# Row normalisation on one core: loading the first tile through two queues, and a new cut of the scale that two engines share

## The chip, the cores and the metric

The kernel runs on one core of one Trainium2 chip. The metric is the device time of one execution in microseconds (us). The record calls two kernels the same when they lie within 2% of each other. Smaller differences are read here from the ratio and its 95% interval.

## The reference

```python
def setup_inputs():
    batch, dim = 1024, 4096
    return {"x": np.random.randn(batch, dim).astype(np.float32),
            "axis": -1, "eps": np.float32(1e-12)}

def reference(x, axis, eps):
    norm = np.sqrt(np.sum(x ** 2, axis=axis, keepdims=True) + eps)
    return (x / norm).astype(np.float32)
```

16.78 MB come in and 16.78 MB go out. There is little arithmetic to each byte.

## The kernel before

The 1024 rows are two tiles of 128 partitions x 4 rows x 4096 columns, 8.39 MB each, with 64 KB in every partition. The four rows of a partition are called rows 0 to 3 here. Both loads and both stores go through one queue, that of SyncE.

```python
    for i in range(n_tiles):
        g = RowGroups(nc, io, stats, scratch, D, R, eps_t)
        load = nc.sync.dma_start(out=g.flat(), in_=x_t[i])
        if i == 0:
            first_load_to_front(nc, load.ins)   # ahead of the entry barrier
        groups.append(g)

    for i, g in enumerate(groups):
        g.square_dve(R - 1)          # row 3: VectorE
        g.square_act(0)              # rows 0, 1, 2: ScalarE
        g.norm(0)                    # root on ScalarE, reciprocal on VectorE
        g.scale(0)                   # VectorE
        ...                          # the same for rows 1 and 3
        g.square_act(2)
        g.norm(2)
        if i < n_tiles - 1:
            g.scale_by_both(2)       # tile 0: both engines, cut at 7/8
        else:
            g.scale(2)
        store = nc.sync.dma_start(out=out_t[i], in_=g.flat())
```

```python
    def scale_by_both(self, r):
        cut = 7 * self.D // 8
        rstd = self.rstd[:, r : r + 1]
        self.nc.scalar.activation(out=self.x[:, r, :cut], in_=self.x[:, r, :cut],
                                  func=ACT_F.Copy, scale=rstd)
        self.nc.vector.tensor_scalar_mul(out=self.x[:, r, cut:],
                                         in0=self.x[:, r, cut:], scalar1=rstd)
```

`first_load_to_front` moves the finished instruction into the entry block, ahead of SyncE's drain, and so ahead of the barrier at which the engines meet before the body of the kernel: in the trace this load's issue starts at 0.00 us, the second load's, behind the barrier, at 0.79.

## Time and profile before

| | before |
|---|---|
| time, median of 3 runs | 81.94 us (81.75 to 81.99) |
| span of the profiled execution | 80.2 us |
| VectorE, ScalarE busy | 33%, 37% |
| share of the 16 DMA engines' time in packets | 97.4% |
| first store issued / load 1 landed | 38.99 us / 41.37 us |

The time is about 1.8 us longer than the span, which runs from the first to the last instruction. A transfer counts as landed when all 16 DMA engines have reported; the trace has 16 reports for each. The views behind the table stand in the prediction below, with what is to be seen in them.

### The profile page before, as it was taken

The numbers are of one execution on the slowest core, as the hardware profiler recorded it, in microseconds if no ns is written. First come the engines' busy times: TensorE is split into PE (matmuls) and PEld (weight loads), VectorE is DVE, ScalarE is ACT, GpSimd is POOL, SyncE is SP. The second block draws the span as 40 slices with busy tenths as digits, with TensorE's granted clock in tenths as the row PEclk, the third lists the DMA queues.
The fourth block names the chain that finished last, engine by engine and source line by source line (L and its number), as shares of the span: only waits on it lengthen the run. The fifth ranks groups of instructions, "written<-read, shape, count | busy, mean of one in ns | idle before, by whom it ended". The sixth has DMA issues, their size and how long they took to land.

```text
span 80.2 us, 93 instructions
## 1 busy us (share of the span) xinstructions
DVE 26.7 (33%) x21; ACT 29.7 (37%) x23; POOL 0.2 (0%) x4
## 2 busy tenths in 40 slices
DVE  0000000000099599960039995999200000000000
ACT  6000000000099999989439999950000000000000
POOL 0000000000000000000000000000000000000000
DMA  9099996699996699996699990999991999992990
GB/s 490 33 523 523 523 490 294 261 523 523 523 490 261 294 523 523 523 490 261 294 523 523 523 490 33 523 523 523 523 458 65 523 523 523 523 425 98 523 523 0
DMA packets 576, 33.55 MB, mean 418 GB/s; under 512 B 64, under 2 KB 64, under 8 KB 64
## 3 DMA queue, kind: packets, MB, share of 16 engines
q1 hardware_dynamic: 576, 33.55, 97.4%
HBM read 16.78 MB, written 16.78 MB: 418 GB/s over the span
## 4 chain that ended last, share of the span: by engine, by line
DMA 51%; ACT 10%; DVE 9%; issue 0%
DMA xt<-in_x_dram 51%; ACT sq_act L33 9%; DVE xt L64 9%; ACT rstd L53 1%; DVE rstd L59 0%
## 5 line engine op out<-in xcount | busy, mean ns | idle before, releaser
L33 ACT ACTIVATE sq_act<-xt 128x4096 f32<-128x4096 f32 x6 | 21.7, 3609 | 22.4 <-DMA xt<-in_x_dram 22.4
L42 DVE SCALAR_TENSOR_TENSOR sq_dve<-xt 128x4096 f32<-128x4096 f32 x2 | 8.9, 4426 | 26.4 <-DMA xt<-in_x_dram 26.4
L64 DVE TENSOR_SCALAR xt<-xt,rstd 128x4096 f32<-128x4096 f32 x7 | 16.5, 2353 | 0.2
L72 ACT ACTIVATE xt<-xt,rstd 128x3584 f32<-128x3584 f32 x1 | 3.3, 3283 | 0.2 <-DVE rstd L59 0.2
L53 ACT ACTIVATE rstd<-ssq,eps_t 128x1 f32<-128x1 f32 x8 | 2.1, 290 | 0.1
L59 DVE RECIPROCAL rstd<-rstd 128x1 f32<-128x1 f32 x8 | 1.3, 160 | 2.5 <-ACT rstd L53 2.5
L33 ACT ACT_TABLE_LOAD x1 | 1.3, 1283 | 0.8 <-PEq L258 0.8
L53 ACT ACT_TABLE_LOAD x1 | 1.3, 1283 | 0.0
L33 ACT ACTIVATION_READ_ACCUMULATOR sq_act<-xt 128x1 f32 x6 | 1.1, 187 | 0.0
L78 DVE TENSOR_SCALAR xt<-xt,rstd 128x512 f32<-128x512 f32 x1 | 0.5, 487 | 0.0
L211 DVE MEMSET eps_t<- 128x1 f32 x1 | 0.1, 59 | 0.9 <-PEq L258 0.9
L42 DVE DVE_READ_ACCUMULATOR sq_dve<-xt 128x1 f32 x2 | 0.2, 83 | 0.0
L258 POOL MEMSET const-uint8-127<- 128x1 uint8 x1 | 0.1, 103 | 0.0
L258 POOL MEMSET const-bfloat16-1.0<- 128x1 bf16 x1 | 0.1, 102 | 0.0
L258 POOL MEMSET const-float32-0.0<- 128x1 f32 x1 | 0.1, 99 | 0.2 <-issue 0.2
L258 POOL MEMSET const-float32-1.0<- 128x1 f32 x1 | 0.1, 99 | 0.0
## 6 DMA issues: line engine op xcount, KB each, us to landing
xt<-in_x_dram SPq DMA_DIRECT2D x2, 31.3
out_dram<-xt SPq DMA_DIRECT2D x2, 22.5
```

The lines of the kernel that those rows point to most:

```text
L33: self.nc.scalar.activation(out=sq_a, in_=self.x[:, r], func=ACT_F.Square, accum_out=self.ssq[:, r : r + 1],)
L42: self.nc.vector.scalar_tensor_tensor(out=sq_v, in0=self.x[:, r], scalar=1.0, in1=self.x[:, r], op0=ALU.mult, op1=ALU.mult, accum_out=self ...
L53: self.nc.scalar.activation(out=self.rstd[:, r : r + n], in_=self.ssq[:, r : r + n], func=ACT_F.Sqrt, bias=self.eps_t,)
L59: self.nc.vector.reciprocal(out=self.rstd[:, r : r + n], in_=self.rstd[:, r : r + n])
L64: self.nc.vector.tensor_scalar_mul(out=self.x[:, r], in0=self.x[:, r], scalar1=self.rstd[:, r : r + 1])
L72: self.nc.scalar.activation(out=self.x[:, r, :cut], in_=self.x[:, r, :cut], func=ACT_F.Copy, scale=rstd,)
L78: self.nc.vector.tensor_scalar_mul(out=self.x[:, r, cut:], in0=self.x[:, r, cut:], scalar1=rstd)
L211: nc.vector.memset(eps_t, eps)
L258: nc = _bacc.Bacc("TRN2", target_bir_lowering=False, num_devices=1)
```

## The change

The intent: use both issuing engines for the first tile, so that it arrives sooner, and rebalance the shared scale so that the first store can go out sooner.

```diff
-        cut = 7 * self.D // 8
+        cut = 3 * self.D // 4
...
-            if i.engine == mybir.EngineType.SP and isinstance(i, mybir.InstDrain)
+            if i.engine == load.engine and isinstance(i, mybir.InstDrain)
...
-        load = nc.sync.dma_start(out=g.flat(), in_=x_t[i])
         if i == 0:
-            first_load_to_front(nc, load.ins)
+            half = R * D // 2
+            for queue, part in ((nc.sync, slice(half)), (nc.scalar, slice(half, None))):
+                load = queue.dma_start(out=g.flat()[:, part], in_=x_t[i][:, part])
+                to_front(nc, load.ins)
+        else:
+            nc.sync.dma_start(out=g.flat(), in_=x_t[i])
```

The first half holds rows 0 and 1, the second rows 2 and 3.

More of the change, by code (lines that the diff above doesn't have):

```diff
@@ L80, in scale_by_both, with to_front @@
         )
-def first_load_to_front(nc, load):
+def to_front(nc, load):
     def move(program):
```

## The prediction

So is the term for the added packets in the sum: the sum came to about -0.15 us, and so to 81.8 us, with that term in it; the two terms left to read (-0.2 and -0.05) don't add up to that. That the DMA engines take the two halves packet by packet in turn, on which the landing of the halves and the first rival rest, was an assumption: the trace of before has one queue and can't show it. How the descriptors of the two halves are prepared (second rival) and what the start consists of (third rival) are conjectures too. In the trace of before 16 packets of 65,536 bytes in 2.418 us are 433.7 GB/s; that a second queue leaves this rate as it is was assumed as well.

> **What bounds the kernel now.** I read the page first: the busy shares, the slices, the DMA queue.
>
> ```profile
> span 80.2 us, 93 instructions
> DVE 26.7 (33%) x21; ACT 29.7 (37%) x23; POOL 0.2 (0%) x4
> q1 hardware_dynamic: 576, 33.55, 97.4%
> HBM read 16.78 MB, written 16.78 MB: 418 GB/s over the span
> ```
>
> No compute engine is busy for even two fifths of the span, while the packets fill 97.4% of the time of the 16 DMA engines. Two loads and two stores of 8.39 MB each follow one another on one queue, so this is a copy with arithmetic hidden in it. All that isn't copying is 2.6% of 80.2 us, about 2.1 us; no change that leaves the bytes alone can win more than that.
>
> Next I wanted to know whether the four transfers follow without a hole. The view of tile xt and that of the output give the times from issue to landing:
>
> ```profile
> L219 SPq DMA_DIRECT2D xt<-in_x_dram x2: 333/358/383, 0.0 to 0.8; - x2
> DMA to landing us min/median/max: 22.1/31.3/40.6
> L240 SPq DMA_DIRECT2D out_dram<-xt x2: 343/346/348, 39.0 to 56.8; - x2
> DMA to landing us min/median/max: 21.7/22.5/23.3
> ```
>
> The loads are issued at 0.0 and 0.8 and land at 22.1 and 41.4; the stores are issued at 39.0 and 56.8 and land at 60.7 and 80.0. The steps between landings are 19.3, 19.3 and 19.3 us. Every engine moves 8 packets of 64 KB per transfer, and a packet of the steady part takes 2.418 us in the trace's packet records: 8 x 2.418 = 19.34. So three of the four steps are pure copying, and the first holds 22.1 - 19.3 = 2.8 us of start.
>
> The packet records of the first microseconds show what that start is. On eleven of the 16 engines the first packet starts between 1.0 and 1.2 us, on the others between 1.5 and 2.1. Most of these first packets take 2.5 to 3.4 us in place of 2.42, and they end between 4.02 and 4.80. From there each engine runs on: 4.80 + 31 x 2.418 = 79.76, and the records have the last engine ending at 79.69, landed at 80.03. The end is thus set by the engine whose first packet ended last, as long as no hole comes later.
>
> The one place where a hole could come is the first store. The timeline around it:
>
> ```profile
> 22.08 3.62 ACT L33 ACTIVATE sq_act<-xt 128x4096 f32<-128x4096 f32 x1 [20.01 <-DMA xt<-in_x_dram]
> 22.09 4.42 DVE L42 SCALAR_TENSOR_TENSOR sq_dve<-xt 128x4096 f32<-128x4096 f32 x1 [21.16 <-DMA xt<-in_x_dram]
> ...
> 35.68 3.28 ACT L72 ACTIVATE xt<-xt,rstd 128x3584 f32<-128x3584 f32 x1 [0.23 <-DVE rstd L59]
> 35.68 0.49 DVE L78 TENSOR_SCALAR xt<-xt,rstd 128x512 f32<-128x512 f32 x1
> 38.99 18.11 SPq L240 DMA_DIRECT2D out_dram<-xt  x2
> 41.40 3.62 ACT L33 ACTIVATE sq_act<-xt 128x4096 f32<-128x4096 f32 x1 [2.43 <-DMA xt<-in_x_dram]
> ```
>
> Tile 0 lands at 22.08; ScalarE's chain of squares, roots and the shared scale ends at 38.97, and the store is issued at 38.99. The reader is to see that this is only 2.4 us before load 1 has landed. In the packet records the engines finish load 1 between 40.3 and 41.1, and the store's packets cannot start before about 40.5 to 40.7, which is 1.5 to 1.7 us after the issue. Four engines therefore idle for 0.2 to 0.5 us there; the last engine does not. The transfer is just in time: spare time about 0.3 us, none on four engines. Tile 1 has more: its store is issued at 56.8 and waits behind store 0, which lands at 60.7.
>
> [...]
>
> **The change part by part.** *Two halves on two queues.* One issue of 64 KB a partition becomes two of 32 KB, one from ScalarE, whose first real instruction, the table load, starts at 0.79 us after the entry barrier. ScalarE idles for 20 us after it, so an issue of about 0.4 us ahead of the barrier costs nothing there. SyncE already does the same and reaches the barrier in time (its drain ends at 0.57, the release comes at 0.71). The bytes are the same. There are 128 more packets, 8 per engine: [...] What can be won is part of the start: with two queues filling, an engine that gets its first packet late (1.97 and 2.12 us) may get one earlier from the other queue. If the slowest first work ended at the mean of the others' (about 4.4 for 4.80), 0.4 us are won. I count half, 0.2 us, as nothing shows that the two issues are prepared side by side rather than in turn.
> *Landing of the halves.* If the engines alternate strictly, rows 0 and 1 land one 32 KB packet (1.2 us) before rows 2 and 3, and ScalarE's chain, which starts with row 0, starts up to 1.2 us earlier. That moves the store's issue forward, onto spare time.
> *Shared scale at 3/4.* ScalarE 3072 elements for 3584: [...] 0.43 less. VectorE 1024 for 512: by the rows of 4096 (2353 ns) and 512 (487 ns) an element costs 0.52 ns, so 754 ns, 0.27 more, beside ScalarE and far shorter. The store is issued 0.43 us sooner. That closes the holes of 0.2 to 0.5 us on four engines, none of which ends last: worth about 0 in the span, up to 0.1 through jitter. It also is insurance for the store if tile 0 lands later.
> The sum: -0.2 (start) [...] - 0.05 (holes) = about -0.15 us, so 81.94 - 0.15 = 81.8.
>
> **Rivals.** *First rival: the second half lands late.* Load 1 is issued on SyncE's queue right behind the first half. If ScalarE's half lags by one packet on one engine, a 64 KB packet of load 1 comes in before the last packet of tile 0, which then lands 2.4 us later, at 24.5. VectorE squares row 3 first, for 4.42 + 0.08 us: 24.5 to 29.0, and one of ScalarE's two roots at 27.1 to 27.6 needs that row. The rest of ScalarE's chain, 27.1 to 38.97 = 11.9, less 0.43, then ends at 29.0 + 11.5 = 40.5, the store's packets start at 42.1, and engines that were free at 41.1 at the latest idle for about 1 us: 83.0. For it: both engines start in the same 0.1 us, so a small lag decides; and a landing counts only when all 16 engines are done. [...] If in addition row 0 waited for both halves, the chain would be 2.4 - 0.43 = 2.0 late, and the time about 83.5; against that, the two halves of the shared scale start together at 35.68, so parts of a tile are tracked apart.
> *Second rival: the descriptors of both halves are prepared in turn.* Then the last engine's first packet starts later than 2.1 us, by up to the 1.1 us over which the first starts are spread now: 82.5 to 83. Against: an engine needs only one packet of either half to be busy.
> *Third rival: hidden anyway.* The start is the latency of the first reads, whoever asks; the first packets still end between 4.0 and 4.8, and the time is 81.9. The stretched first packets on eleven engines that started together speak for it.
> *A compute engine becoming the bound* I rule out: both are under 40%.
>
> **Range and chances.** I give the main line and the third rival together 65% (81.4 to 82.0), the first rival 20%, the second 15%. That puts the middle at 81.8, and eight cases in ten between 81.3 and 82.9. Faster by over 2% means under 80.3, which would take 1.6 of the 2.1 us that aren't copying: 2%. Slower by over 2% means over 83.6, the first rival at its worst: 5%. Within 2%: 93%.
>
> **What the changed profile would show.** Right: a second DMA queue with 4.19 MB, the share still at 97% or above; first packets ending no later than 4.8 us; the shared scale at 2.86 us on ScalarE and 0.75 on VectorE; the store issued before 38.6; landings still 19.3 us apart. Wrong: rows 2 and 3 landing near 24.5, VectorE's first square starting 2 us after ScalarE's, a store issued after 40 and a step of more than 20 us between load 1 and store 0 (first rival); a first landing after 22.5 with all later steps unchanged (second rival). The prediction fails upward if the halves don't interleave evenly, and downward only if the start falls by more than half of its 2.8 us.

## The result, and the profile after

The changed kernel took 81.90 us (median of 6 runs, 81.81 to 82.10), the kernel before 81.94 (6 runs, 81.72 to 82.02). The ratio is 1.0003, with a 95% interval of 0.9985 to 1.002: the same. (A ratio is the mean time of one kernel's fast runs over that of the other's of the same rounds, so it isn't quite the ratio of the medians.)

The page of the changed kernel, to be laid beside the lines of before:

```profile
span 80.0 us, 97 instructions
DVE 27.0 (34%) x21; ACT 29.3 (37%) x23; POOL 0.2 (0%) x4
q1 hardware_dynamic: 576, 29.36, 85.4%
q10 hardware_dynamic: 144, 4.19, 12.1%
HBM read 16.78 MB, written 16.78 MB: 419 GB/s over the span
```

A second queue, q10, now carries 4.19 MB, but the two shares add up to 97.5%, where one queue had 97.4%: the same engines are as full as before. The timeline of the changed kernel:

```profile
0.00 0.38 SPq L222 DMA_DIRECT2D xt<-in_x_dram  x1
0.12 0.36 ACTq L222 DMA_DIRECT2D xt<-in_x_dram  x1
...
21.90 3.62 ACT L33 ACTIVATE sq_act<-xt 128x4096 f32<-128x4096 f32 x1 [19.71 <-DMA xt<-in_x_dram]
22.08 4.42 DVE L42 SCALAR_TENSOR_TENSOR sq_dve<-xt 128x4096 f32<-128x4096 f32 x1 [21.04 <-DMA xt<-in_x_dram]
...
35.49 2.85 ACT L72 ACTIVATE xt<-xt,rstd 128x3072 f32<-128x3072 f32 x1 [0.23 <-DVE rstd L59]
35.49 0.75 DVE L78 TENSOR_SCALAR xt<-xt,rstd 128x1024 f32<-128x1024 f32 x1
38.37 18.59 SPq L244 DMA_DIRECT2D out_dram<-xt  x2
41.26 3.62 ACT L33 ACTIVATE sq_act<-xt 128x4096 f32<-128x4096 f32 x1 [2.92 <-DMA xt<-in_x_dram]
```

Both issues stand ahead of the barrier (0.00 and 0.12 us; the issue of load 1, behind it, starts at 0.91). ScalarE starts on rows 0 and 1 at 21.90, VectorE on row 3 at 22.08. The first store goes out at 38.37, 0.62 us sooner than before, and yet load 1 lands at 41.24 (before: 41.37) and the last instruction ends at 80.03 (before: 80.20).

The packet records of the trace show how the halves come to arrive together. They don't name the engine, so each packet was joined to the one that ended where it begins; where engines stood idle that isn't unambiguous, and sums and means are given for them below. Each line is one of the 16 engines, S a packet of SyncE's queue and A one of ScalarE's, with the size in KB and start and end in us:

```
S32@1.00-2.69  A32@2.69-3.90  S32@3.90-5.11 ...  S32@18.41-19.62  A32@19.62-20.83  S64@20.84-23.26
S32@1.03-3.28  A32@3.28-4.50  S32@4.49-5.71 ...  S32@19.00-20.22  A32@20.21-21.43  S64@21.43-23.85
```

In these records all 16 engines take strict turns on tile 0, S and A, with 1.21 us for each packet but the first. The last S packet of the tile ends between 19.6 and 20.3 us. The next record of SyncE's queue, a 4-byte packet taken here for its report, doesn't follow there, though: on every engine it stands behind the A packet, between 20.83 and 21.49, within 0.01 us of the other queue's 4-byte record. The halves count as landed at 21.88 and 22.06, with the last of their 16 reports. The 1.2 us between the halves' last packets shrink to 0.18 us between their landings. What holds the first report back, the runs don't show.

### The profile page after: what moved, and what is told of

The parts are those of the page before. It is cut to its first block, busy times and chain, and to the rows that moved or that the text cites. A ratio compares the mean times of both kernels' runs of the same rounds, so it can differ in the third digit from the quotient of the medians.

```text
span 80.0 us, 97 instructions
## 1 busy us (share of the span) xinstructions
DVE 27.0 (34%) x21; ACT 29.3 (37%) x23; POOL 0.2 (0%) x4
## 3 DMA queue, kind: packets, MB, share of 16 engines
q10 hardware_dynamic: 144, 4.19, 12.1%
## 4 chain that ended last, share of the span: by engine, by line
DMA 50%; ACT 10%; DVE 9%; issue 0%
DMA xt<-in_x_dram 50%; ACT sq_act L33 9%; DVE xt L64 9%; ACT rstd L53 1%; DVE rstd L59 0%
## 5 line engine op out<-in xcount | busy, mean ns | idle before, releaser
L72 ACT ACTIVATE xt<-xt,rstd 128x3072 f32<-128x3072 f32 x1 | 2.9, 2855 | 0.2 <-DVE rstd L59 0.2
L78 DVE TENSOR_SCALAR xt<-xt,rstd 128x1024 f32<-128x1024 f32 x1 | 0.8, 753 | 0.0
```

What stands on the lines that cost most here:

```text
L78: self.nc.vector.tensor_scalar_mul(out=self.x[:, r, cut:], in0=self.x[:, r, cut:], scalar1=rstd)
```

## The experiments

Each edit is to the changed kernel, unless the text says otherwise. Three questions: does each part alone do something (the two could cancel), what does the second queue give, and why does an earlier store not help? The theory at first was the prediction's: the copy fills the DMA engines (97.4%) and everything else is hidden, apart from the start.

### The split alone, and the cut alone

```diff
 # the split alone: the changed kernel with
-        cut = 3 * self.D // 4
+        cut = 7 * self.D // 8
 # the cut alone: the kernel before with
-        cut = 7 * self.D // 8
+        cut = 3 * self.D // 4
```

> The two halves on two queues, the shared scale left at 7/8. Theory (the start is the latency of the first reads [...], all else is hidden): within 0.3 us of the kernel before, 81.6 to 82.2; rows 0 and 1 land less than 0.3 us before rows 2 and 3, near 21.9 and 22.1; the first store is issued near 38.8 (0.18 us sooner than before, as row 0 lands sooner), and the last engine ends between 79.3 and 79.8. Rival (the parts cancel: the split wins at the start and the new cut gives it back): 81.4 or less.

> One load as before, the shared scale at 3/4. Theory: 81.9, within 0.3 us; ScalarE's part 2.86 us, the first store issued near 38.56 in place of 38.99, and the holes of 0.2 to 0.5 us on four engines between load 1 and store 0 gone or under 0.1 us; the last engine still ends near 79.7. Rival (the parts cancel): this one is slower than before by the same amount that the split alone is faster.

The split alone: 81.91 us beside 81.82 for the kernel before in the same rounds, ratio 1.0015 (1.0001 to 1.0029), store issued at 38.76. The cut alone: 82.06, ratio 1.0032 (1.0019 to 1.0045), store issued at 38.21. Neither gains, so the idea that two effects cancel falls. But the cut alone costs 0.2 us, more than the scatter, though it only issues the store sooner. In its records the last packets of load 1 took up to 3.00 us instead of 2.42, on 13 of the 16 engines over 2.46. That was not foreseen.

```profile
38.21 18.90 SPq L240 DMA_DIRECT2D out_dram<-xt  x2
41.41 3.62 ACT L33 ACTIVATE sq_act<-xt 128x4096 f32<-128x4096 f32 x1 [3.23 <-DMA xt<-in_x_dram]
```

### No arithmetic at all

All calls between loads and stores are taken out. The inputs come back.

```diff
-        g.square_dve(R - 1)
-        g.square_act(0)
-        ... (to the end of the scale)
         store = nc.sync.dma_start(out=out_t[i], in_=g.flat())
```

> The changed kernel without any arithmetic: the outputs are the inputs, wrong on purpose. Each store waits for its load alone. Theory (all compute is hidden): 81.8 to 82.0, as fast as either kernel, the four landings 19.3 us apart. Rival (a part of the chain of compute still shows): faster by 0.5 us or more.

83.04 us, ratio 1.0154 (1.0140 to 1.0167): both the theory (81.8 to 82.0) and its rival (faster) are wrong. A bare copy is 1.2 us **slower** than the copy with the arithmetic. Its timeline holds one line for the stores:

```profile
21.91 20.68 SPq L229 DMA_DIRECT2D out_dram<-xt  x2
```

The first store is issued at 21.91, as soon as tile 0 is in, and then stands in the queue behind load 1 for some 19 us. In the records all packets of load 1 take 2.42 us, except the last one on every engine, the one just ahead of the store: 3.30 to 3.90 us. Load 1 lands at 42.24, and the later steps follow at their usual distances. There is no idle time; a packet has become longer.

### Both halves on one queue

```diff
-for queue, part in ((nc.sync, slice(half)), (nc.scalar, slice(half, None))):
+for queue, part in ((nc.sync, slice(half)), (nc.sync, slice(half, None))):
```

> Both halves ahead of the barrier, but both on SyncE's queue: what two transfers do without the second queue. Theory: rows 0 and 1 land near 12.2 (8 packets of 1.21 us after a start of 1.9, a receipt of 0.4) and rows 2 and 3 near 21.9; ScalarE starts near 12.2 and then waits for row 3's square, so the first store goes out near 37.9 or sooner; the time is still 81.9, within 0.3 us. Rival (the second queue itself wins at the start): 0.2 us or more slower than the kernel with two queues.

```profile
12.06 3.62 ACT L33 ACTIVATE sq_act<-xt 128x4096 f32<-128x4096 f32 x1 [9.51 <-DMA xt<-in_x_dram]
...
31.62 26.46 SPq L244 DMA_DIRECT2D out_dram<-xt  x2
42.38 3.62 ACT L33 ACTIVATE sq_act<-xt 128x4096 f32<-128x4096 f32 x1 [11.08 <-DMA xt<-in_x_dram]
```

With one queue the first half does land ahead, at 12.03, and the store goes out at 31.62. The time is 83.08 us, ratio 1.0155 (1.0141 to 1.0169). By the expectations that would speak for the rival (the second queue gains at the start). But the start is no later here: the first packets end such that the slowest engine reaches full speed at 2.01 us (the end of its first packet less the packet's steady duration), against 2.14 in the changed kernel and 2.38, 2.06 and 2.18 in three profiles with one undivided load. What is different is again the last packet of load 1, 3.20 to 3.88 us. The runs thus suggest a new theory: **a store that is queued too early stretches the last packet ahead of it.** Its rival is that the missing arithmetic and the single queue each cost 1.1 us for reasons of their own.

### A better balance of the shared scale

Cut at one half, the two engines finish closer together (2.00 us on ScalarE and 1.29 on VectorE in its profile, 2.85 and 0.75 in the changed kernel's), and the store can go out sooner still. By the new theory that makes the kernel slower.

```diff
-        cut = 3 * self.D // 4
+        cut = self.D // 2
```

> The changed kernel with the shared scale cut at one half: ScalarE 2048 elements (2.00 us), VectorE 2048 (1.29 us), so the first store is issued near 37.5, 0.85 us sooner. Theory formed on the first four runs (a store that is queued before the engines are nearly through load 1 stretches load 1's last packet, by 0 when issued at 38.4 to 39 and by 0.9 to 1.5 us when issued at 31.6 or 21.9): slower, by 0.3 to 1.1 us, 82.2 to 83.0; the last packets of load 1 take 2.8 to 3.9 us in place of 2.42. Rival (issuing sooner can't hurt; the two slow runs were slow for another reason, the removed compute or the single queue): 81.9.

82.50 us, ratio 1.0081 (1.0064 to 1.0098), as the new theory said. Its timeline:

```profile
37.46 20.30 SPq L244 DMA_DIRECT2D out_dram<-xt  x2
42.06 3.62 ACT L33 ACTIVATE sq_act<-xt 128x4096 f32<-128x4096 f32 x1 [4.63 <-DMA xt<-in_x_dram]
```

The store is issued 0.91 us sooner than in the changed kernel, and load 1 lands 0.80 us later (42.04 for 41.24). Load 1 was queued before 1.3 us in both and nothing else in it was altered. The last packets of load 1 took 2.84 to 3.39 us.

### More work, on purpose

This is the decisive one. The kernel with both halves on one queue gets three useless multiplications by 1.0 ahead of its first store, and nothing else:

```diff
 # the kernel with both halves on one queue
+        if i == 0:
+            for _ in range(3):
+                nc.vector.tensor_scalar_mul(
+                    out=g.x[:, R - 1], in0=g.x[:, R - 1], scalar1=1.0)
         store = nc.sync.dma_start(out=out_t[i], in_=g.flat())
```

> The kernel with both halves on one queue, which issued its first store at 31.6 and took 83.1 us, with three useless multiplications by 1.0 on VectorE ahead of that store (3 x 2.35 us), so that it is issued near 38.6. Theory (the time of the issue decides: too soon stretches load 1's last packet): the stretch is gone, and the kernel with 7 us more work is faster, 81.7 to 82.2. Rival (the single queue or the halves cost the 1.1 us): still 83.0 to 83.2.

```profile
38.51 18.22 SPq L249 DMA_DIRECT2D out_dram<-xt  x2
41.03 3.62 ACT L33 ACTIVATE sq_act<-xt 128x4096 f32<-128x4096 f32 x1 [9.82 <-DMA xt<-in_x_dram]
```

Seven microseconds of added work (6.95 in the timeline) bring the time from 83.08 down to 81.83 us (ratio to the kernel before 0.9997, 0.9984 to 1.0011). The store moves from 31.62 to 38.51, load 1's last packets are back at 2.42 to 2.43 us, and it lands at 41.01. Here the moment of the issue decides, not the queue or the halves.

### The late edge

One useless activation of 2048 elements ahead of the shared scale, once in the kernel before and once in the changed one (2.00 us in both timelines):

```diff
         rstd = self.rstd[:, r : r + 1]
+        self.nc.scalar.activation(
+            out=self.scratch["act"][:, :2048], in_=self.x[:, r, :2048],
+            func=ACT_F.Square, scale=rstd)
         self.nc.scalar.activation(
```

> The kernel before with one useless activation of 2048 elements [...] ahead of the shared scale: the store is issued near 40.9. Theory of the late edge: its first packets start 1.5 to 1.7 us after the issue, near 42.5, the engines, free from 40.3 to 41.1, idle 1.4 to 2.2 us, and the time is 83.2 to 83.6. Rival (there is more slack than that): 82.3 or less.

> The same useless activation in the changed kernel: the store is issued near 40.3, 0.6 us sooner than in the kernel before with it, packets from 41.9, the time 82.5 to 83.0. Theory: here the two savings (0.18 us of landing, 0.43 us of scale) are worth their full 0.6 us, as they lie on the path; rival: the difference to the other late kernel is under 0.3 us.

```profile
40.79 16.12 SPq L246 DMA_DIRECT2D out_dram<-xt  x2
```

```profile
40.50 16.54 SPq L250 DMA_DIRECT2D out_dram<-xt  x2
```

The first line is the kernel before with the delay: 83.06 us (ratio 1.0148), a little under the expected 83.2; the 16 engines idle for 1.2 us on average between load 1 and the store. The second is the changed kernel with it: 82.65 us (1.0096), idle for 0.85 us on average. The difference is 0.41 us, less than the 0.6 expected. It is the size of the cut's saving (3283 - 2855 ns = 0.43 us); the 0.18 us of the landing are missing. In these two profiles tile 0 landed at 21.84 with one load, and its first half at 21.97 with two, so the sooner landing of the result section was scatter.

The first kernel came out under its expectation because the prediction's figure of 1.5 to 1.7 us from issue to first packet, which that expectation used, doesn't hold here. It was read from engines that got through load 1 only 1.3 to 1.5 us after the issue. In the late kernels every engine was through within 0.41 us of it, and the store's first packets start 0.84 to 0.99 us after it (41.64 to 41.78 for an issue at 40.79).

The runs line up by the time at which the first store was issued:

| run | store issued, us | last packet of load 1, median (longest), us | idle engines at the store, us | time, us | ratio |
|---|---|---|---|---|---|
| no arithmetic | 21.91 | 3.60 (3.90) | none | 83.04 | 1.0154 |
| one queue | 31.62 | 3.66 (3.88) | none | 83.08 | 1.0155 |
| cut at 1/2 | 37.46 | 3.14 (3.39) | none | 82.50 | 1.0081 |
| cut alone | 38.21 | 2.58 (3.00) | none | 82.06 | 1.0032 |
| changed | 38.37 | 2.42 (2.55) | none | 81.90 | 1.0003 |
| one queue, more work | 38.51 | 2.42 (2.43) | none | 81.83 | 0.9997 |
| split alone | 38.76 | 2.42 (2.42) | three, 0.5 in all | 81.91 | 1.0015 |
| before | 38.99 | 2.43 (2.43) | five, 1.1 in all | 81.94 | 1 |
| changed, late | 40.50 | 2.42 (2.42) | all, 0.85 each on average | 82.65 | 1.0096 |
| before, late | 40.79 | 2.42 (2.42) | all, 1.2 each on average | 83.06 | 1.0148 |

This is a valley with a flat floor from about 38.4 to 39.0 us. The kernel before lay at its right edge and the changed kernel lies at its left edge. Load 1's last packets start near 38.1 and end near 40.5, so on the floor that packet is already under way. The left edge isn't sharp: with the cut alone the last packets began between 37.85 and 38.28, the store was issued at 38.21, and 13 of them were stretched a little. The times of issue come from one profile each, the ratios from 4 to 6 runs, so the edges are known to a few tenths of a microsecond at best.

### Loads and stores in turn

Does the cost belong to every change from a load packet to a store packet? The bare copy with its first store on ScalarE's queue makes each engine alternate between load 1 and store 0:

```diff
 # the kernel without arithmetic
-        store = nc.sync.dma_start(out=out_t[i], in_=g.flat())
+        queue = nc.scalar if i == 0 else nc.sync
+        store = queue.dma_start(out=out_t[i], in_=g.flat())
```

> The copy without arithmetic (wrong on purpose), with the first store on ScalarE's queue, so that each engine alternates packets of load 1 and of store 0 for 40 us. If each change from a load packet to a store packet costs the 1.1 us that the early store cost: some 7 more changes on each engine, 7 to 9 us more than the copy in order (83.0), about 91. If the cost arises once for a transfer, or only where both stand in one queue: 82 to 83.5. If loads and stores share the engine better than either alone: under 81.

```profile
22.19 0.35 ACTq L230 DMA_DIRECT2D out_dram<-xt  x1
58.97 0.35 SPq L230 DMA_DIRECT2D out_dram<-xt  x1
```

83.55 us, ratio 1.0209 (1.0191 to 1.0227): near the second expectation, far from the 91 of a cost for every change. One engine of the trace:

```
S64@20.93-23.35  S64@23.35-26.84  A64@26.84-29.26  S64@29.25-31.67  A64@31.67-34.08 ...
```

The packet just ahead of the first store packet is stretched (2.8 to 3.6 us over the engines); the alternation after it runs at 2.42 us a packet. So here the cost comes once, with the beginning of a store that is queued well ahead behind a load, and not with each change. (In the late kernels a store that begins on idle engines has first packets of 2.45 to 2.46 us.) The second store, issued at 58.97 when its queue had run empty, again has a long packet, its own first (2.7 to 3.5 us). In the kernel before and the changed one the second store, queued behind the first, shows none (its longest packet takes 2.44 us). What the engine does in that microsecond, no run here shows.

### The start

```diff
                 load = queue.dma_start(out=g.flat()[:, part], in_=x_t[i][:, part])
-                to_front(nc, load.ins)
```

> The changed kernel with both halves left behind the entry barrier. Theory (the start is paid in full by the span): both issues start near 0.75 in place of 0.0 and 0.12, and all later times move by 0.7 to 0.8 us, the first store with them, so its place against load 1 stays; 82.6 to 82.8. Rival (the start is hidden or belongs to something else than the issue): 82.2 or less.

```profile
0.73 0.39 ACTq L222 DMA_DIRECT2D xt<-in_x_dram  x1
0.73 0.38 SPq L222 DMA_DIRECT2D xt<-in_x_dram  x1
...
39.20 18.58 SPq L243 DMA_DIRECT2D out_dram<-xt  x2
```

82.71 us, ratio 1.0101 (1.0083 to 1.0119): 0.73 us of later issue cost 0.8 us. In this run the start is paid in full. The store moves along with the load (39.20 for 38.37), so the valley isn't left. By that measure a gain at the start would have shown.

To see what the long first packets are, the first 512 columns became a transfer of their own:

```diff
-for queue, part in ((nc.sync, slice(half)), (nc.scalar, slice(half, None))):
+for queue, part in ((nc.sync, slice(512)), (nc.scalar, slice(half, None)),
+                    (nc.sync, slice(512, half))):
```

> The changed kernel with the first 512 columns (2 KB a partition) as a transfer of their own ahead of the rest of the first half: what the long first packets are. Theory (a fixed latency of the first reads): the first packets of 2 KB still take 0.6 us or more each on most engines in place of 0.08, full speed is reached near 1.9 us as before, and the time is within 0.3 us of 81.9. Rival (the delay grows with the packet, so small ones start the flow sooner): full speed before 1.5 us and a time under 81.6.

82.12 us, ratio 1.0035 (1.0019 to 1.0050), and a miss in its expectation: the very first 2 KB packets of most engines took 0.08 to 0.35 us, not 0.6 or more, so a fixed latency of each first packet isn't the whole story. Nor did they help, as the 32 KB packets of the other queue began only at 2.0 to 3.1 us. The run has a second fault: ScalarE's table load came only behind its wait for the tile (at 22.28 us in the timeline, at 0.91 in the changed kernel's), so the store went out at 40.05, past the right edge of the valley. It says nothing clean about the time; the cause of the long first packets stays open.

### A second half that lags

For the prediction's first rival, ScalarE's transfer is held up until its table load and a one-element activation into its own destination are through:

```diff
             half = R * D // 2
+            nc.scalar.activation(out=g.x[:, 2, 0:1], in_=eps_t, func=ACT_F.Square)
...
-                to_front(nc, load.ins)
+                if queue is nc.sync:
+                    to_front(nc, load.ins)
```

> The second half is made late: ScalarE's transfer waits for a one-element activation into its own destination behind the table load, so it is issued near 2.4 us. First rival of the prediction: on the engines where it lags by a packet or more, a 64 KB packet of load 1 comes in before its last packet, rows 2 and 3 land near 24.3 or later, the first store is issued at 40 or later, the engines idle for about 1 us, the time is 82.7 to 83.5. Other view (the halves alternate all the same, as the first packet lasts until 3 us): rows 2 and 3 land near 22.1 and the time is 81.9.

```profile
2.31 0.36 ACTq L223 DMA_DIRECT2D xt<-in_x_dram  x1
18.12 3.62 ACT L33 ACTIVATE sq_act<-xt 128x4096 f32<-128x4096 f32 x1 [15.85 <-DMA xt<-in_x_dram]
...
29.02 4.43 DVE L42 SCALAR_TENSOR_TENSOR sq_dve<-xt 128x4096 f32<-128x4096 f32 x1 [28.11 <-DMA xt<-in_x_dram]
...
43.62 15.56 SPq L246 DMA_DIRECT2D out_dram<-xt  x2
```

The four executions took 85.73, 85.80, 87.78 and 88.02 us. The record marks the last two as slow, at the same granted clock of 1.0; they weren't profiled. The two fast ones, at about 85.8, give the ratio 1.0475 (1.0452 to 1.0498). What that rival describes happened here, and larger than I sized it: issued 2.2 us later, the second half fell three packets behind on each engine (the records read S S S S A S A), so packets of load 1 came in between, and rows 2 and 3 landed at 28.99. The store went out at 43.62 and the engines idled for 4 us. The roots also stand in another order in this build (one alone at 23.14 and two together at 33.49 us; in the changed kernel the first two go together at 26.93), so the 43.62 isn't due to the landing alone.

No version tried beats both kernels: the best, at 81.83 us, has a ratio of 0.9997 to the kernel before.

## Why the prediction was right

The call, 81.8 us and the same within 2%, held, and what carried it was its first step: the copy fills 97.4% of the engines' time, so about 2 us at most could be won, an estimate that takes the 2.418 us of a packet as given (the changed kernel's packets, too, take 2.418 in the median). That 81.8 came within 0.1 us of the result is luck as far as the forecast saving of 0.15 us goes: the measured ratio has an interval of about 0.15 us to either side and its middle is no change, and the third rival's 81.9 fits better. The signs listed for a right prediction came true (97.5% in two queues, the store at 38.37, landings 19.2 to 19.3 us apart), but they don't separate the main line from that rival. The steps fared unevenly.

- **The parts' costs.** 2.86 us and 754 ns were given for the shared scale; 2855 and 753 ns were measured. From 3584 to 3072 elements ScalarE's part fell by 428 ns, from 512 to 1024 VectorE's rose by 266.
- **The start (-0.2 us).** Not shown. The slowest engine reached full speed at 2.14 us in the changed kernel, and over the other profiles at 2.00 to 2.30 with two queues and 1.90 to 2.38 with one. The third rival, that the start is the same whoever asks, is what fits the runs, and with issues moved by 0.73 us the time moved by 0.8.
- **The added packets.** In the records a steady 32 KB packet takes 1.213 us, so two of them take 0.008 us more than one of 64 KB (2.418), which is 0.06 us over the eight pairs of the tile.
- **The landing of the halves ("up to 1.2 us earlier").** Wrong. The engines do alternate strictly in the records of tile 0, but the 4-byte record of the first half comes only behind the other queue's packet (20.83 to 21.49 us): the gain is 0.18 us in the changed kernel, and less than the scatter over the profiles.
- **Moving the store "onto spare time", as insurance.** This step failed. I took an early store to be free. Issued 0.9 us sooner than in the changed kernel it costs 0.6 us, and at 31.6 or sooner it costs 1.2. The change moved the store from one edge of a valley to the other, so its saving of 0.43 us on ScalarE had nothing to be worth.
- **The holes.** Closed, as said, though the records show five idle engines (1.1 us in all) and not four. The engine that starts the store last, at 41.05, is not among them and ends last, so nothing came of it.
- **Issue to first packet (1.5 to 1.7 us).** It was read rightly from the kernel before, but it is no fixed latency: 0.84 to 0.99 us in the two late kernels. The first rival's 83.0 used it, and would have come out lower with the shorter figure.
- **The first two rivals.** The lag of a packet didn't happen, with issues 0.12 us apart; forced, it cost 3.9 us (the fast executions). Preparation of the two halves in turn was to show in a last first packet later than 2.1 us; it starts at 1.94 in the changed kernel.

## What to carry to other kernels

When transfers fill the engines, look for the time at which each is queued, not only for when its data is ready: here a store queued much too soon behind a load (at 31.62 us, 83.08 us in all) cost as much as one queued nearly two microseconds late (at 40.79, 83.06 us), and added work that moved it to 38.51 cured it (81.83 us). Splitting a load over two queues brought no earlier half here, where both halves took turns on the same 16 engines (landings at 21.88 and 22.06 us); on one queue the first half landed at 12.03. Before rewarding a rebalanced engine, ask what the instruction after it waits for, and measure a part alone when the sum is zero.
